# Five warming matmuls in front of the first product, earlier low parts, and other due times in a hybrid decoder layer

## The chip, the cores and the metric

The kernel runs on one core of a Trainium2 chip. The metric is the device time of one execution in microseconds (us). It is measured in several runs, of which the median counts, and once more under the hardware profiler. The engines are named as in the profile: PE (TensorE, its matmuls), PEld (its weight loads), DVE (VectorE), ACT (ScalarE), POOL (GpSimd) and SP (SyncE, which issues most DMAs).

## What is computed

One decoder layer on 512 tokens of width 1024, in float32:

```python
mod = silu(c) @ w_mod + b_mod
shift, scale, gate = split(mod, 3)
h = rmsnorm(x, norm_gain) * (1 + scale) + shift
q, k, v, z_attn, x_lru, z_lru = split(h @ w_in)          # 512 columns each
attn = moba_attention(rope(q), rope(k), v)               # 8 heads x 64; with 512 tokens: causal
y_attn = rmsnorm(attn, attn_out_gain) * silu(z_attn)
rec = rg_lru(causal_depthwise_conv(x_lru))               # gates, then a linear recurrence over time
y_lru = rmsnorm(rec, lru_out_gain) * silu(z_lru)
out = rmsnorm(x + gate * (concat(y_attn, y_lru) @ w_out), final_gain)
```

## The kernel before

Every large product is done with split operands: a number is kept as a rounded part (its name ends in h, type fp32r) and the rest (ends in l), and a product is three matmuls: high by high, low by high, high by low. `split` (L247) issues the high part as a copy, on ACT or DVE, and the low part as a subtraction on DVE.

**The opening.** The input x comes as four tiles of 128 tokens. ACT squares and sums each (L349), and the row is scaled by its inverse norm: the first 256 columns at once (`xs`, L358 and L361), the other 768 later (`x`, L358), not before the time in the table `REST`. The projection's first seven column blocks (q, k and x_lru, `NFIRST`) are accumulated in seven PSUM banks (`acc`) over the eight steps d of the contraction, 128 channels each. For step d:

- two dots on DVE (`gain`, L385 for d = 0, L397 after) take rows of w_mod times silu(c) (`cb`) and give the shift and the scale of these channels; two small instructions (L402, L405) combine them into the columns of `g`. For d > 0 they read `vec`, a table of vectors that a DMA brings, to whose scale columns 1 is added once (L369, on DVE).
- four transposes on PE (L413 from `x`, L417 from `xs` for d = 0) put the tokens along the free axis, in the bank `xp`.
- two ACT instructions (L420) read `xp` and apply `g`: `hh` (rounded) and `h` (full). A subtraction on DVE (L422) gives `hl`.
- the weights' 896 columns are split (`w0dh`, `w0dl`). For d = 0 they come as two pieces of 512 and 384 columns, split apart (`w00512h`, `w00384h` and their low parts).
- 21 matmuls on PE (L432): seven columns by three passes, `hh` with the high weights, `hh` with the low weights, `hl` with the high weights.

Ahead of the first product, matmuls on a constant tile (`warm`) run into a spare bank (`spare`, L312): 24 of them, `NWARM`. PSUM has eight banks, and a tile keeps its bank from its first writer to its last reader.

**The rest.** PE goes through the other column blocks (`UNITS`: x3, four blocks of v, k and q of the second head group, the gates a0 to a3 and l0 to l3), each as 24 matmuls (L243 to L245) into a bank `pj`. Between them stand the attention (scores `sc` L588, softmax on DVE and ACT L601 to L616, transposes `tp` L651, products with v `av` L634) in six blocks, three for each group of four heads, and the recurrence (convolution, gates, `decay`; then `recur`, L547 to L549: a square root on ACT, a product and a scan on DVE for each of four channel blocks). At the end come the output products (`po`, also L243 to L245), the residual and the final norm.

**What sets the order.** The kernel doesn't issue instructions as the code is read. `op` records each with its engine, a cost, what it reads and writes, and a due time or none. `Plan.emit` first works due times back: an operation's due time is the least of its own and, for each that reads its result, that one's due time less its cost and a latency. Then it walks through time by its own clock: on each engine it takes of the operations that could start within 0.12 us of the first the one that is due soonest, adding 4.1 to the due time of an ACT operation that would change the activation table. A tile gets a buffer only when one is free, and no sooner than a window ahead of its due time. The parameter `after` holds an operation back to a time of that clock. What comes out is one fixed order per engine, which the chip follows, waiting on semaphores.

Constants that the change touches: `SPACE` is the distance of the due times of two attention blocks; the second group's first is due at 122.88 on the planner's clock whatever `SPACE` is. `REC0` is the due time of the first recurrence after `T_REST` (50.2). `T_FIRST` (11.8) is the due time of the first product; that of step d is 4.79 d later.

Of the kernel before, what the change touches and what calls it, by code (L numbers as in the profile page):

```python
# [7 lines left out]
F32 = mybir.dt.float32  # L8
F32R = mybir.dt.float32r
BF16 = mybir.dt.bfloat16  # L10
AF = mybir.ActivationFunctionType
OP = mybir.AluOpType
# [5 lines left out]
ND = D // 128  # L18
# [1 line left out]
BIG = 3.0e38  # L20
LRU_C = 8.0
NFIRST = 7
NWARM = 24
CUTS = (((0, 768), (768, 1024)), ((0, 512), (512, 1024)))
REST = (14.6, 14.7, 17.2, 17.3)

V_GAIN, V_SHIFT, V_SCALE, V_GATE = 0, 8, 16, 24
V_CW, V_CB, V_BR, V_BI, V_LAM, V_AG, V_LG = 32, 48, 52, 56, 60, 64, 68
V_C = 72
NV = 80  # L30
UNITS = ["x3", "v0", "v1", "v2", "v3", "k2", "k3", "q2", "q3", "a0", "a1", "l0", "l1", "l2", "l3", "a2", "a3"]
SPACE = 13.0
BY_TANH = ("a0", "a1", "a2", "a3", "l0", "l1", "l2", "l3")
GATE0, GATE_STEP, DECAY0, REC0 = 32.0, 3.0, 56.0, 84.0


class Buf:
# [23 lines left out]
class Plan:  # L61
# [11 lines left out]
    def op(self, eng, cost, fn, r=(), w=(), due=None, table=None, lat=0.25, after=0.0, alt=None):  # L73
        o = Op(eng, cost, fn, list(r), list(w), due, table, lat, after, alt)
        deps = set()
        for b in o.r:
            if b.writer is not None:
                deps.add(b.writer)
        for b in o.w:
            if b.writer is not None:  # L80
                deps.add(b.writer)
            deps.update(b.readers)
        for b in o.r:
            b.readers.append(o)
        for b in o.w:
            b.writer, b.readers = o, []
        for b in set(o.r) | set(o.w):
            b.users += 1
        deps.discard(o)
        o.deps = list(deps)  # L90
        for d in deps:
            d.outs.append(o)
        o.left = len(deps)
        self.ops.append(o)
        return o
# [82 lines left out]
def tile_hymba_block(ctx: ExitStack, tc: tile.TileContext, x, ws0, wss, wgt, win0, wv, winr,  # L178
                     wo, wg, vecs, top, fgain, consts, out):
    nc = tc.nc  # L180
    V, A, G, PE, SP = nc.vector, nc.scalar, nc.gpsimd, nc.tensor, nc.sync
# [19 lines left out]
    op = plan.op  # L201

    def t2(name, dt=F32):
        return Buf("t2", [128, 512], dt, name)

    def t4(name, dt=F32, shape=(128, 1024)):
        return Buf("t4", list(shape), dt, name)

    def bank(name, kind=None):
        return Buf("ps", [128, 512], F32, name, kind)  # L210
# [4 lines left out]
    def fix(name, shape, dt=F32):  # L215
        return Buf("fix", list(shape), dt, name)


    def dv(n, ptr=0):
        return 0.075 + n / 960.0 + 0.06 * ptr  # L220
# [4 lines left out]
    def ac(n, ptr=0, acc=0):  # L225
        return 0.09 + n / 1200.0 + 0.1 * ptr + 0.1 * acc

    def acp(n, ptr=0, acc=0):
        return ac(n, ptr, acc) - 0.039

    def copy(n, dst, src, r, w, due=None, psum=False, after=0.0):

        op("A", acp(n) if psum else ac(n), lambda: A.copy(dst(), src()), r, w, due, after=after,  # L233
           alt=("V", dv(n) if psum else dv2(n), lambda: V.tensor_copy(dst(), src())))

    def pe(n, passes=1):
        return passes * n / 2250.0
# [9 lines left out]
    def split(src, new, name, n, due=None, scale=None, behind=(), late=()):  # L247
        hi, lo = new(name + "h", F32R), new(name + "l", F32R)
        if scale is None:
            copy(n, lambda: hi[:], lambda: src[:], [src, *behind], [hi], due)  # L250
            op("V", dv(n), lambda: V.tensor_sub(lo[:], src[:], hi[:].bitcast(F32)), [src, hi, *late], [lo], due)
        else:
            op("A", ac(n), lambda: A.activation(hi[:], src[:], AF.Copy, scale=scale), [src], [hi], due)
            op("V", dv(n), lambda: V.scalar_tensor_tensor(lo[:], src[:], scale, hi[:].bitcast(F32),
                                                          op0=OP.mult, op1=OP.subtract), [src, hi], [lo], due)
        return hi, lo

    def like(t):
        return lambda name, dt: t4(name, dt, t.shape)


    def t_first(d):
        return T_FIRST + 4.79 * d

    T_FIRST, T_REST, STEP = 11.8, 50.2, 0.94

    def t_step(n):
        return T_REST + STEP * n
# [5 lines left out]
    vec, ident, cst = fix("vec", [128, NV]), fix("ident", [128, 128]), fix("cst", [128, 2048])  # L274
# [34 lines left out]
    warm, spare = t2("warm", BF16), bank("spare")  # L309
    op("V", 0.3, lambda: V.memset(warm[:], 1.0), [], [warm], -10)  # L310
    for n in range(NWARM):
        op("PE", 0.32 if n < 11 else 0.235, lambda: PE.matmul(spare[:], warm[:, 0:128], warm[:], start=True, stop=True),  # L312
# [3 lines left out]
    epsc, ones, junk = fix("epsc", [128, 1]), fix("ones", [128, 1]), fix("junk", [128, 1])  # L316
# [28 lines left out]
    for t in range(NT):  # L345
# [6 lines left out]
        if t > 1:  # L352
            op("V", 0.1, lambda ss=ss: V.reciprocal(ss[:, 0:1], ss[:, 1:2]), [ss], [ss], due + 0.3)
        for dst, cut, e, due2, after in ((xs[t], slice(0, 256), "VVAA"[t], due + 0.4, 0.0), (xt[t], slice(256, D), "A", 20.0 + t, REST[t])):
            o = (lambda d_, c_: d_[:] if d_ in xs else d_[:, c_])
            n = cut.stop - cut.start
# [3 lines left out]
            else:  # L360
# [4 lines left out]
    h = [t2(f"h{d}") for d in range(ND)]  # L365
    hh = [t2(f"h{d}h", F32R) for d in range(ND)]
    hl = [t2(f"h{d}l", F32R) for d in range(ND)]
    acc = [bank(f"acc{j}") for j in range(NFIRST)]
    op("V", 0.1, lambda: V.tensor_scalar(vec[:, V_SCALE:V_SCALE + ND], vec[:, V_SCALE:V_SCALE + ND], 1.0, None,  # L369
                                         op0=OP.add), [vec], [vec], t_first(1) - 3)  # L370

    sch = col("sch")

# [34 lines left out]
    for d in range(ND):  # L408
        g, xp = gain(d), bank(f"xp{d}")

        def turn(xp=xp, d=d):
            for t in range(NT):
                PE.transpose(xp[:, t * 128:(t + 1) * 128], (xt if d > 1 else xs)[t][:, d * 128:(d + 1) * 128], ident[:])  # L413
        if d:
            op("PE", 0.44, turn, (xt if d > 1 else xs) + [ident], [xp], t_first(d) - 3.8)
        for t in range(NT if not d else 0):
            op("PE", 0.11, lambda t=t, xp=xp: PE.transpose(xp[:, t * 128:(t + 1) * 128], xs[t][:, 0:128], ident[:]),  # L417
               [xs[t], ident], [xp], 7 + 0.5 * t)
        for o in (hh[d], h[d]):
            op("A", acp(512, 2), lambda o=o, d=d, xp=xp, g=g: A.activation(  # L420
                o[:], xp[:], AF.Identity, bias=g[:, 0:1], scale=g[:, 1:2]), [xp, g], [o])
        op("V", dv(512), lambda d=d: V.tensor_sub(hl[d][:], h[d][:], hh[d][:].bitcast(F32)), [h[d], hh[d]], [hl[d]])  # L422
        if d:
            wp = [split(w0[d], like(w0[d]), f"w0{d}", 128 * NFIRST)] * 2
        else:
            wp = [split(w, lambda name, dt, w=w: Buf("t2", w.shape, dt, name), w.name, w.shape[1], late=[g],
                        behind=[hh[0]] if w is w0[0][1] else []) for w in w0[0]]
        for i, (a, b) in enumerate(((0, hh[d]), (1, hh[d]), (0, hl[d]))):
            for j in range(NFIRST):
                w, k = wp[j // 4][a], j if d else j % 4  # L430
                op("PE", pe(512), lambda w=w, k=k, b=b, j=j, first=(d == 0 and i == 0), last=(d == ND - 1 and i == 2):
                   PE.matmul(acc[j][:], w[:, k * 128:(k + 1) * 128], b[:], start=first, stop=last),  # L432
                   [w, b], [acc[j]], t_first(d) + (0.62 if d else 1.6) * i + 0.21 * j)
# [290 lines left out]
    for j in range(8):  # L724
# [3 lines left out]
    att = [(g, b) for g in range(2) for b in ((0, 1), (2,), (3,))]  # L728
    t_att = [T_REST + 10.0 + SPACE * n if n < 3 else
             max(t_step(8 * (UNITS.index("q3") + 1)) + 5.0, T_REST + 10.0 + SPACE * 3) + SPACE * (n - 3) for n in range(6)]  # L730
    done = 0
# [57 lines left out]
    for g in range(4):  # L789
# [6 lines left out]
        for j in range(2):  # L796
            w = t4(f"wo{g}{j}", F32, (128, 2, 512))
# [4 lines left out]
        for t in range(NT):  # L802
# [3 lines left out]
            for n, (lo, up) in enumerate(zip(cuts, cuts[1:])):  # L806
                ps, w = bank("po"), up - lo
# [30 lines left out]
                if last and not n:  # L838
# [5 lines left out]
                                                           bias=ssq[t][:, 0:1], scale=1.0 / D), [n4], [n4], t1 + 0.3, "sqrt")  # L844
                op("V", 0.1, lambda t=t: V.reciprocal(ssq[t][:, 3:4], ssq[t][:, 3:4]), [n4], [n4], t1 + 0.4)
                done_a, done_b = Buf("view", None), Buf("view", None)
                for to, up, mark in ((outa[t], 512, done_a), (outb[t], 512, done_b))[:1 if last else 2]:
                    fns = dict(A=lambda t=t, to=to, up=up: A.activation(to[:, :up], to[:, :up], AF.Copy, scale=ssq[t][:, 3:4]),
                               V=lambda t=t, to=to, up=up: V.tensor_scalar(to[:, :up], to[:, :up], ssq[t][:, 3:4], None, op0=OP.mult))
# [86 lines left out]
```

## Time and profile before

| | us |
|---|---|
| three runs | 235.19, 233.93, 235.91 |
| median | 235.19 |
| the profiled execution | 236.3 |
| its span, from the first to the last instruction | 234.2 |

The profile is of one execution. Its page gives busy time for each engine and the granted clock of TensorE in 40 slices; its trace answers for single instructions: when one started, how long it took, and what ended the idle time before it (in square brackets). A matmul's time in a timeline holds its way through the array and so overlaps the next one's; what a matmul costs is the distance of starts. The same holds, by about 0.1 us, for ACT and DVE.

### The profile page before, as it was taken

The page shows a single profiled execution, that of the slowest core. Times are in us where ns is not written, and L with a number is a line of the kernel's source. Part 1 is how long each engine was busy: PE and PEld are TensorE (multiplying, and loading weights), DVE is VectorE, ACT ScalarE, POOL GpSimd, SP SyncE. Part 2 cuts the span into 40 slices and gives each one's busy share as a digit, 9 for nine tenths or more (in the row PEclk, how much of TensorE's full clock was granted, in tenths as well). Part 3 has the DMA queues.
Part 4 walks back from the last instruction along what each step waited for, and adds up shares of the span by engine and source line. Part 5 has one row for each costly group of instructions (what it writes and reads, how often), then busy time and mean ns, then how long its engine had stood idle before and what let it go on. Part 6 is the DMA issues. An engine that isn't in the chain of part 4 may idle for free.

```text
span 234.2 us, 3421 instructions
## 1 busy us (share of the span) xinstructions
PE 224.5 (96%) x1221; PEld 178.2 (76%) x1221; DVE 203.7 (87%) x396; ACT 150.0 (64%) x277; POOL 9.6 (4%) x32
## 2 busy tenths in 40 slices
PE   7969999999999999999999999999999999999990
PEld 3458888888888787686888788778886788888890
DVE  1699998886999997999999999899989999975582
ACT  7888565643549968599998886894763723032363
POOL 1010000067000000000000000000000000000000
PEclk9979999999999999999999999999999999999998
DMA  6999999841270450534322247347450000000044
GB/s 230 395 401 411 404 409 416 347 118 65 71 260 30 179 179 24 206 133 164 108 89 91 94 155 293 96 136 300 189 179 3 0 0 0 3 0 0 0 179 181
DMA packets 11782, 38.27 MB, mean 163 GB/s; under 512 B 1515, under 2 KB 1782, under 8 KB 11638
## 3 DMA queue, kind: packets, MB, share of 16 engines
q1 hardware_dynamic: 11600, 37.80, 43.5%
q10 hardware_dynamic: 166, 0.27, 0.3%
q8 instruction: 9, 0.15, 0.2%
q14 instruction: 7, 0.06, 0.1%
HBM read 35.96 MB, written 2.10 MB: 162 GB/s over the span
## 4 chain that ended last, share of the span: by engine, by line
PE 91%; DMA 3%; DVE 2%; ACT 1%; SPq 1%; issue 0%; ACTq 0%
PE acc L432 17%; PE pj L243 14%; PE pj L245 13%; PE pj L244 13%; PE po L243 6%; PE po L245 6%; PE po L244 6%; PE av L634 4%; PE sc L588 4%; PE tp L651 4%; DMA ws<-in_ws_dram 3%; PE g L511 1%; PE xp L413 1%; DVE ws L385 1%; PE ss L779 1%; SPq L240 1%
## 5 line engine op out<-in xcount | busy, mean ns | idle before, releaser
L604 ACT ACTIVATE z<-z,mn 128x128 f32<-128x128 f32 (+3 forms) x32 | 17.8, 558 | 7.6 <-DVE mn L601 7.5
L397 DVE SCALAR_TENSOR_TENSOR ws<-ws,cb 128x1024 f32<-128x1024 f32 x14 | 16.9, 1221 | 0.5 <-DMA ws<-in_wss_dram 0.5
L601 DVE CUSTOM_DVE_ANT_0 z<-sc,cst 128x128 f32<-128x128 f32 (+3 forms) x32 | 14.3, 486 | 0.9 <-PE pj L244 0.5
L233 ACT COPY pt<-tp 128x128 f32<-128x128 f32 (+3 forms) x28 | 9.7, 405 | 5.5 <-PE tp L651 5.4
L828 ACT ACTIVATE o<-xr 128x512 f32<-128x512 f32 x7 | 4.4, 634 | 12.0 <-DVE xr L817 12.0
L817 DVE SCALAR_TENSOR_TENSOR xr<-po,rba,xr 128x512 f32<-128x512 f32 (+2 forms) x9 | 6.2, 691 | 5.9 <-PE po L245 5.7
L651 PE MATMUL tp<-ident,z 128*128 128x128 f32 x80 | 10.4, 272 | 0.0
L651 PEld LDWEIGHTS tp<-ident,z 128*128 128x128 f32 x80 | 9.3, 141 | 1.3
L799 DVE TENSOR_TENSOR wo<-wo,grow 128x1024 f32<-128x1024 f32 x8 | 9.8, 1219 | 0.0
L559 DVE SCALAR_TENSOR_TENSOR wgt<-wgt,cb 128x1024 f32<-128x1024 f32 x8 | 9.7, 1218 | 0.0
L634 PE MATMUL av<-pt,v 128*64 128x256 f32 (+3 forms) x64 | 9.3, 436 | 0.0
L312 PE MATMUL spare<-warm 128*128 128x512 bf16 x24 | 7.8, 468 | 1.5 <-DVE ones L318 1.5
L634 PEld LDWEIGHTS av<-pt,v 128*64 128x64 f32 x64 | 5.4, 137 | 4.1 <-issue 2.2
L496 DVE SCALAR_TENSOR_TENSOR xc<-xl,vec,xc 128x511 f32<-128x511 f32 (+2 forms) x12 | 8.4, 745 | 0.1
L616 DVE TENSOR_SCALAR z<-z,sum 128x128 f32<-128x128 f32 (+3 forms) x20 | 7.2, 383 | 0.4
L675 ACT ACTIVATE sz<-pj 128x512 f32<-128x512 f32 x8 | 4.8, 599 | 3.7 <-PE pj L245 3.1
L615 ACT ACTIVATE z<-z,sum 128x128 f32<-128x128 f32 (+3 forms) x12 | 6.4, 556 | 0.7 <-DVE sum L612 0.7
L817 DVE SCALAR_TENSOR_TENSOR xr<-po,rbl,xr 128x512 f32<-128x512 f32 x8 | 6.0, 748 | 0.3 <-PE po L245 0.2
L420 ACT ACTIVATE h<-xp,g 128x512 f32<-128x512 f32 x8 | 6.2, 771 | 0.0
L604 ACT ACTIVATION_READ_ACCUMULATOR z<-z,mn 128x1 f32 x32 | 6.1, 190 | 0.0
L312 PEld LDWEIGHTS <-warm 128*128 128x128 bf16 x24 | 2.5, 113 | 4.2 <-DVE ones L318 1.5
L523 DVE COPY gr<-g 64x512 f32<-64x512 f32 x6 | 4.1, 688 | 1.7 <-ACT gi L519 1.6
(1100 smaller groups left out, 752.3 us busy)
## 6 DMA issues: line engine op xcount, KB each, us to landing
wc<-in_winr_dram SPq DMA_DIRECT2D x13, 512.0 KB, 3.4
ws<-in_wss_dram SPq DMA_DIRECT2D x4, 1024.0 KB, 12.1
wgt<-in_wgt_dram SPq DMA_DIRECT2D x8, 512.0 KB, 3.7
wo<-in_wo_dram SPq DMA_DIRECT2D x8, 512.0 KB, 4.2
w<-in_win_dram SPq DMA_DIRECT2D x7, 448.0 KB, 9.5
ws<-in_wss_dram SPq DMA_DIRECT2D x6, 512.0 KB, 6.6
x<-in_x_dram SPq DMA_DIRECT2D x4, 512.0 KB, 5.3
wv<-in_wv_dram SPq DMA_DIRECT2D x4, 512.0 KB, 6.8
```

Source lines behind the costliest of these rows:

```text
L243: PE.matmul(ps, lh, rh, start=start, stop=False)
L244: PE.matmul(ps, lh, rl, start=False, stop=False)
L245: PE.matmul(ps, ll, rh, start=False, stop=stop)
L312: op("PE", 0.32 if n < 11 else 0.235, lambda: PE.matmul(spare[:], warm[:, 0:128], warm[:], start=True, stop=True), [warm], [spare], 5.3 + ...
L397: op("V", dv(1024), lambda j=j: V.scalar_tensor_tensor(part(d, j), part(d, j), 1.0, cb[:], op0=OP.mult, op1=OP.mult, accum_out=sc[:, j:j + ...
L432: PE.matmul(acc[j][:], w[:, k * 128:(k + 1) * 128], b[:], start=first, stop=last),
L601: op("V", dv(n) + 0.085, lambda s=s, z=z, mn=mn: V.tensor_tensor_reduce(out=z[:, :n], in0=ps[s][:, cut], in1=cst[:, 2048 - n:2048], op0=OP ...
L604: op("A", ac(n, 1, 1), lambda s=s, z=z, mn=mn, sm=sm: A.activation(z[:, :n], z[:, :n], AF.Exp, bias=mn[:, 0:1], scale=-1.0, accum_out=sm[: ...
L634: PE.matmul(pss[u][64 * s:64 * s + 64, k * 128:], vt[k][:, h * 64:h * 64 + 64], pts[2 * u + s][:, k, k * 128:], start=(k == 0), stop=(k == 3))
L651: PE.transpose(at(h)[:, k * 128:(k + 1) * 128], z[:, k * 128:(k + 1) * 128], ident[:])
L799: op("V", dv(1024), lambda w=w, s=s: V.tensor_mul(w[:], w[:], grow[:, None, s].to_broadcast([128, 2, 512])), [w, grow], [w], t0 - 7 + 2 * j)
L817: op("V", dv(w, 1), lambda t=t, ps=ps, c0=c0, c1=c1, br=br: V.scalar_tensor_tensor(res[t][:, c0:c1], ps[:, :c1 - c0], rb[br][:, t:t + 1], ...
```

## The change

- `NWARM` goes from 24 to 26, and five more warming matmuls (`NLATE`) are recorded behind the transposes of step 1 (they read its bank `xp`), due from 11.1 on the planner's clock.
- `REST`: the 768 columns of the third and fourth x tile are scaled no sooner than 18.2 and 18.3 on the planner's clock, instead of 17.2 and 17.3.
- The addition of 1 to the scale columns of `vec` goes from DVE (a tensor_scalar) to ACT (an activation with a bias column of ones), due 1 us later.
- `hl` of step 0 gets a due time of 12.5, and the split of the two weight pieces of step 0 one of 12.0; before, these had only what followed from the products.
- `SPACE` goes from 13.0 to 12.6, and `REC0` from 84 to 80.

```diff
@@ -20,18 +20,18 @@
 BIG = 3.0e38
 LRU_C = 8.0
 NFIRST = 7
-NWARM = 24
+NWARM, NLATE = 26, 5
 CUTS = (((0, 768), (768, 1024)), ((0, 512), (512, 1024)))
-REST = (14.6, 14.7, 17.2, 17.3)
+REST = (14.6, 14.7, 18.2, 18.3)
 
 V_GAIN, V_SHIFT, V_SCALE, V_GATE = 0, 8, 16, 24
 V_CW, V_CB, V_BR, V_BI, V_LAM, V_AG, V_LG = 32, 48, 52, 56, 60, 64, 68
 V_C = 72
 NV = 80
 UNITS = ["x3", "v0", "v1", "v2", "v3", "k2", "k3", "q2", "q3", "a0", "a1", "l0", "l1", "l2", "l3", "a2", "a3"]
-SPACE = 13.0
+SPACE = 12.6
 BY_TANH = ("a0", "a1", "a2", "a3", "l0", "l1", "l2", "l3")
-GATE0, GATE_STEP, DECAY0, REC0 = 32.0, 3.0, 56.0, 84.0
+GATE0, GATE_STEP, DECAY0, REC0 = 32.0, 3.0, 56.0, 80.0
 
 
 class Buf:
@@ -366,8 +366,8 @@
     hh = [t2(f"h{d}h", F32R) for d in range(ND)]
     hl = [t2(f"h{d}l", F32R) for d in range(ND)]
     acc = [bank(f"acc{j}") for j in range(NFIRST)]
-    op("V", 0.1, lambda: V.tensor_scalar(vec[:, V_SCALE:V_SCALE + ND], vec[:, V_SCALE:V_SCALE + ND], 1.0, None,
-                                         op0=OP.add), [vec], [vec], t_first(1) - 3)
+    op("A", 0.2, lambda: A.activation(vec[:, V_SCALE:V_SCALE + ND], vec[:, V_SCALE:V_SCALE + ND], AF.Identity, bias=ones[:, 0:1]),
+       [vec, ones], [vec], t_first(1) - 2)
 
     sch = col("sch")
 
@@ -416,14 +416,18 @@
         for t in range(NT if not d else 0):
             op("PE", 0.11, lambda t=t, xp=xp: PE.transpose(xp[:, t * 128:(t + 1) * 128], xs[t][:, 0:128], ident[:]),
                [xs[t], ident], [xp], 7 + 0.5 * t)
+        if d == 1:
+            for n in range(NLATE):
+                op("PE", 0.235, lambda: PE.matmul(spare[:], warm[:, 0:128], warm[:], start=True, stop=True), [warm, xp], [spare],
+                   T_FIRST - 0.7 + 0.1 * n, lat=0.0)
         for o in (hh[d], h[d]):
             op("A", acp(512, 2), lambda o=o, d=d, xp=xp, g=g: A.activation(
                 o[:], xp[:], AF.Identity, bias=g[:, 0:1], scale=g[:, 1:2]), [xp, g], [o])
-        op("V", dv(512), lambda d=d: V.tensor_sub(hl[d][:], h[d][:], hh[d][:].bitcast(F32)), [h[d], hh[d]], [hl[d]])
+        op("V", dv(512), lambda d=d: V.tensor_sub(hl[d][:], h[d][:], hh[d][:].bitcast(F32)), [h[d], hh[d]], [hl[d]], None if d else 12.5)
         if d:
             wp = [split(w0[d], like(w0[d]), f"w0{d}", 128 * NFIRST)] * 2
         else:
-            wp = [split(w, lambda name, dt, w=w: Buf("t2", w.shape, dt, name), w.name, w.shape[1], late=[g],
+            wp = [split(w, lambda name, dt, w=w: Buf("t2", w.shape, dt, name), w.name, w.shape[1], 12.0, late=[g],
                         behind=[hh[0]] if w is w0[0][1] else []) for w in w0[0]]
         for i, (a, b) in enumerate(((0, hh[d]), (1, hh[d]), (0, hl[d]))):
             for j in range(NFIRST):
```

## Rows read from the trace of the kernel before

**Rows 1.** The page: busy time by engine, and the granted clock in 40 slices.

```profile
PE 224.5 (96%) x1221; PEld 178.2 (76%) x1221; DVE 203.7 (87%) x396; ACT 150.0 (64%) x277; POOL 9.6 (4%) x32
...
PEclk9979999999999999999999999999999999999998
```

**Rows 2.** Windows: busy time of each engine, 57 to 227 us.

```profile
sum 170.00, PE 170.00 PEld 136.48 DVE 156.36 ACT 111.90 POOL 1.16; mean PE 85.00 PEld 68.24 DVE 78.18 ACT 55.95 POOL 0.58
```

**Rows 3.** Timeline of PE, 9 to 21 us: start, duration, what, idle time before.

```profile
9.48 1.46 PE L312 MATMUL spare<-warm 128*128 128x512 bf16 x6
11.42 0.33 PE L417 MATMUL xp<-ident,xs 128*128 128x128 f32 x1 [0.47 <-ACT xs L358]
...
12.30 0.60 PE L413 MATMUL xp<-ident,xs 128*128 128x128 f32 x4
14.31 2.08 PE L432 MATMUL acc<-h0h,w00512h 128*128 128x512 f32 x4 [1.41 <-ACT h0h L420]
...
17.47 1.12 PE L432 MATMUL acc<-h0h,w00512l 128*128 128x512 f32 x4
...
20.72 0.84 PE L432 MATMUL acc<-h1h,w01h 128*128 128x512 f32 x3
```

**Rows 4.** The chain that ended last: start, length, what; transposes and a step's products.

```profile
22.47 0.44 PE xp L413 x4
22.91 4.80 PE acc L432 x21
```

**Rows 5.** Windows: length; busy PE, PEld, DVE, ACT, POOL; granted clock; DMA share; GB/s.

```profile
14.00:14.50 0.50, 0.19 (x1) 0.19 (x2) 0.10 (x1) 0.50 (x2) 0.00 (x0) 0.59 0.85 337
...
17.00:17.50 0.50, 0.50 (x3) 0.36 (x2) 0.50 (x3) 0.42 (x1) 0.00 (x0) 0.50 1.07 434
```

**Rows 6.** Timeline of ACT, 13 to 19 us.

```profile
13.48 0.78 ACT L420 ACTIVATE h0h<-xp,g 128x512 fp32r<-128x512 f32 x1
...
14.56 0.78 ACT L420 ACTIVATE h<-xp,g 128x512 f32<-128x512 f32 x1
15.24 1.75 ACT L358 ACTIVATE x<-x,ss 128x768 f32<-128x768 f32 x2
17.08 0.94 ACT L233 CAST w01h<-w 128x896 fp32r<-128x896 f32 x1
17.93 0.94 ACT L358 ACTIVATE x<-x,ss 128x768 f32<-128x768 f32 x1
```

**Rows 7.** Timeline of DVE, 13 to 19 us.

```profile
13.16 0.22 DVE L394 SCALAR_TENSOR_TENSOR g<-sc,v,sch 128x1 f32<-128x1 f32 x1
...
16.19 1.22 DVE L397 SCALAR_TENSOR_TENSOR ws<-ws,cb 128x1024 f32<-128x1024 f32 x1
...
17.34 0.69 DVE L422 TENSOR_TENSOR h0l<-h,h0h 128x512 fp32r<-128x512 f32 x1
17.94 0.17 DVE L369 TENSOR_SCALAR vec<-vec 128x8 f32<-128x8 f32 x1
18.14 0.27 DVE L402 TENSOR_SCALAR g<-sc,vec 128x1 f32<-128x1 f32 x1
18.33 0.15 DVE L405 TENSOR_TENSOR g<-sc,vec 128x1 f32<-128x1 f32 x1
```

**Rows 8.** Timelines: ACT's smallest activation; POOL's wait for the data of vec.

```profile
2.74 0.20 ACT L319 ACTIVATE junk<-epsc 128x1 f32<-128x1 f32 x1
...
14.80 1.09 POOL L443 TENSOR_SCALAR spt<-vec 128x4 f32<-128x4 f32 x1 [13.44 <-DMA vec<-in_vecs_dram]
```

**Rows 9.** Timelines of ACT and PE, 123 to 146 us: table loads, z, its transposes.

```profile
123.94 1.28 ACT L547 ACT_TABLE_LOAD   x1
...
134.06 1.28 ACT L604 ACT_TABLE_LOAD   x1
...
143.97 0.40 ACT L615 ACTIVATE z<-z,sum 128x128 f32<-128x128 f32 x1 [0.43 <-DVE sum L612]
...
145.76 0.60 PE L651 MATMUL tp<-ident,z 128*128 128x128 f32 x4
```

## The prediction

> **What bounds the kernel now.** The page comes first: TensorE is busy for 224.5 of 234.2 us, and of the 40 slices only the third shows a granted clock well under full [rows 1]. The windows after the opening say how strict that is: between 57 and 227 us PE is busy 170.00 of 170.00 us, VectorE 156.36 [rows 2]. Past the opening nothing that only reorders other engines can shorten the time; something is to be won only where PE idles or runs slowly, before 20 us. There the timeline of PE is read next [rows 3]. The last six warming matmuls start at 9.48 and end at 10.94. Then PE has only six transposes until 12.90, and nothing at all until 14.31, when h0h is there. The windows show the clock at 0.59 over 14.00 to 14.50, so it fell at about 14.1 (0.41 us of that half microsecond at half clock make 0.59); it is 0.50, the 1.2 GHz level, still from 17.00 to 17.50 [rows 5], and the four products from 17.47 on, in 1.12 us, go at full clock. So the first seven products take 17.47 - 14.31 = 3.16 us, 0.451 each [rows 3]; at full clock 21 of them take 4.80, 0.2286 each [rows 4]. The penalty is 3.16 - 7 x 0.2286 = 1.56 us.
>
> **The change part by part.** (1) *Five late warmings.* They read xp1, so they stand behind its four transposes, which end at 12.90; the next product waits for h0h until 14.31 [rows 3]. At full clock five cost 5 x 0.243 (1.46 over six) = 1.22 at most, so they end by 14.12 and hide in the 1.41 us of idle time. At half clock they cost 5 x 0.451 = 2.26, end at 15.16 and delay the first product by 0.85. As the clock before fell only around 14.1, I take the first: cost 0, and PE stands still for some 0.2 us instead of 1.41. Whether that is enough to hold the clock no row of before can show. What it wins is bounded by 0 (the clock falls all the same) and the whole 1.56; I take 1.56, since the clock stayed up through everything before 10.94, where warmings stood between transposes in the same way.
> (2) *Two more early warmings.* 2 x 0.243 = 0.49 us, in the 0.47 that PE waits ahead of the transpose at 11.42 [rows 3]. Cost 0; at worst the late chain moves by 0.02.
> (3) *The bank of the warmings.* It is now held to about 14.1 instead of 10.9. With two xp banks it leaves five for the first five products; the sixth takes this bank, and the seventh, at 14.31 + 6 x 0.2286 = 15.68, that of xp0, which is read out when the second h has ended, at 14.56 + 0.78 = 15.34 [rows 6]. Cost 0, with 0.34 to spare.
> (4) *Low parts ahead of the second dot.* With due times of 12.0 and 12.5 against 12.87 for that dot (worked back from the products' due times), DVE takes the low part of the second weight piece, then h0l, then the dot. h0l moves from 17.34 to 16.19 [rows 7]; PE, at full clock, wants it at 14.31 + 14 x 0.2286 = 17.51. In the old order it would end at 17.34 + 0.69 = 18.03, and PE would stand for 0.5 us. The dot starts one slot (17.94 - 17.34 = 0.60) later, at 16.79, and lasts a slot of 17.34 - 16.19 = 1.15, to 17.94. The `vec` addition leaves DVE, so the two g instructions follow at once and are done 0.34 later (18.14 to 18.48), at 18.28.
> (5) *The `vec` addition on ScalarE.* The nearest rows are 0.20 for 128x1 and, far above, 0.78 for 128x512 [rows 6, 8]; I take 0.20, since 8 columns are nearer to 1. Behind it are queued two scalings of x and w01h, for which step 1 waits. Its data lands at 14.80, by POOL's wait [rows 8]. Its due time is 13.8 against 11.6 for the second h, so it goes behind that, at 15.24, and waits for nothing. If it stood ahead of the second weight piece, that piece would be there only at about 15.4 (an estimate: 14.80, 0.20, and 0.4 for the piece, half of w01h's 0.85), for the fifth product at 15.22: PE would lose some 0.2.
> (6) *REST.* Scaling of the third and fourth x is held back to 18.2 on the planner's clock, so h1h no longer stands behind the scaling that starts at 17.93 [rows 6]. ACT is free at 15.24 + 0.20 + 1.84 (two x) + 0.85 (w01h) = 18.13, before g1. h1h starts 0.10 behind g1, as h0h did (13.38 to 13.48): at 18.38. The first product came 0.83 after h0h started, so step 1 can start at 19.21; PE is through step 0 at 14.31 + 21 x 0.2286 = 19.11. Step 1 starts at 19.21 instead of 20.72 [rows 3]: **1.51 us earlier**. Late next is thus h1h, by 0.10. The held-back scalings run from 19.7 to 21.4; the transposes of step 2, which need them, stand some ten products into step 1, at 21.5. A miss costs 0.1.
> (7) *The rest of the opening.* From step 2 on each step has 4.80 of products and 0.44 of transposes on PE, and on DVE two dots, g and two low parts, 2 x 1.15 + 0.34 + 0.60 + 1.0 = 4.2 (the 1.0 an estimate, 0.60 x 896/512). PE stays the later of the two. I lose nothing.
> (8) *Pace 12.6, recurrence due at 80.* No instruction is added: the second attention group's blocks get due times 0.4 and 0.8 us earlier, the square roots, products and scans 4 us. Below nothing there are only switches between sorts of matmul: four transposes among products take 0.60 against 4 x 0.11 in a row [rows 9, 4], so a switch saved or added is about 0.2 us. Above, the price is a PE wait, bounded by the last rival. I take 0: PE has no idle time there to give back, and DVE has 13.6 of 170 us free to absorb a new order [rows 2].
>
> The sum is 1.51. The profiled execution took 236.3 us (span 234.2 and 2.1 around it), so it would take 234.8. It lies 1.1 over the median of 235.19; taken from the median, the sum gives **233.7 us**.
>
> **Rivals.** *The penalty is not whole in every run.* If the clock fell later, or not at all, in some executions of before, the median gains less. For it: the three runs lie 1.98 us apart, somewhat more than the penalty of 1.56, and the profiled execution, which has all of it, is the slowest. Against: only that one execution is seen from inside. With half the gain left, 0.75, the time is 234.4.
> The Trainium skill ("TensorE: Matmul & The Clock Gate", Part 1) has a rule that speaks for this rival: the count of slow matmuls at a kernel's start differs between its runs, 6, 11 or 14 in its example. By that rule the seven of the trace are one draw among several; no row here shows a second one.
> *The clock falls all the same.* Five warmings and a pause may not do. Then (1) wins nothing, and the reorder nothing either, since at half clock PE wants h0l no sooner than it had it; if the clock falls before the five end, the first product is up to 0.85 late. 235.2 to 236.0. For it: the clock did fall with six transposes in the gap. Against: the 1.41 us that were empty are filled.
> *Slower: ScalarE changes tables on softmax's path.* Between 123 and 136 us ACT loads a table four times, first for square roots (123.94), last for the exponentials of the second attention group (134.06), at 1.28 each [rows 9]. Square roots that are due 4 us sooner may go one by one, each as its product is ready, with exponentials between: instead of two pairs four, so two more pairs of loads, 4 x 1.28 = 5.12 us. The last z of the first transposes there is ready at 143.97 + 0.40 = 144.37, and PE takes it at 145.76 [rows 9], 1.39 later. PE would wait 5.12 - 1.39 = 3.7: 233.7 + 3.7 = 237.4. From the third added load on (3.84 - 1.39 = 2.45, over 1.51) the change as a whole is slower. Against it: the planner prices a load, and sooner square roots may as well fall together and spare one.
> The Trainium skill ("ScalarE: Activation LUTs", What ACT_TABLE_LOAD costs) gives 2.66 us for a switch, load and drain together; by that the rival would be 243. The trace differs: the load at 123.94 has no gap on either side, so its 1.28 stands.
>
> **How the numbers follow.** Full gain 0.55 (233.7), partial 0.22 (234.4), none 0.14 (235.2 to 236.0), slower through ScalarE 0.09 (237.4). A change of under 1%, 2.35 us, is about what a measurement of this kernel can't tell from none; the bounds are 232.84 and 237.54. The sum lies 0.8 short of the lower one. Only the spread of the runs, or several spared switches, carries the time past it: 0.14, out of the first case. Past the upper one goes only the larger part of the last case: 0.06. The rest, 0.80, is within. The range goes from 232.6 (1.1 under the first case, half the spread of the runs) to 235.5, into the third case; left out are the last case, part of the third and the tail of the first, under 0.2 together.
>
> **What would show it.** Right: five warming matmuls between 12.9 and 14.1; granted clock 1.00 from 14 to 17.5; seven first products in 1.6 us; h0l at 16.2 on DVE, ahead of the second 1024-wide dot; the `vec` row on ACT behind the second h; step 1 at 19.2; PE's last product ending 1.5 us sooner, with PE busy throughout past the opening. Wrong: a clock of 0.50 after 14 us (the third case), a first product later than 14.31, PE waiting past 57 us for z or for a low part, or more than four table loads on ACT between 120 and 140.

## The result, and the profile after

The changed kernel takes 234.01 us (median of 20 runs, 233.35 to 234.41), the kernel before, measured again beside it, 235.66 (20 runs, 233.93 to 237.89). The ratio is 0.9931, 95% interval 0.9917 to 0.9945: 1.65 us less, where 1.51 was forecast. Runs over 1.5% above the fastest of their kernel count as slow and stand in no ratio: here two of before (237.65 and 237.89; without them it is 1.6 us less), below two of g1. Among the others the scatter fell as well, from 2.53 to 1.06 us, and that turned out to be the more telling number. The profiled execution took 234.14 us, its span 232.1 against 234.2.

The page after, busy time and granted clock in 40 slices, answers to [rows 1]: the 7 in the third slice is gone.

```profile
PE 224.1 (97%) x1228; PEld 176.6 (76%) x1228; DVE 203.1 (88%) x395; ACT 149.8 (65%) x278; POOL 9.6 (4%) x32
...
PEclk9999999999999999999999999999999999999996
```

The timeline of PE after, for [rows 3]: the five warmings (L421) start at 12.65 and end at 13.89, and only 0.33 us are left idle.

```profile
9.29 1.89 PE L312 MATMUL spare<-warm 128*128 128x512 bf16 x8
11.33 0.33 PE L417 MATMUL xp<-ident,xs 128*128 128x128 f32 x1
...
12.65 1.24 PE L421 MATMUL spare<-warm 128*128 128x512 bf16 x5
14.22 1.19 PE L436 MATMUL acc<-h0h,w00512h 128*128 128x512 f32 x4 [0.33 <-ACT h0h L424]
...
15.95 1.08 PE L436 MATMUL acc<-h0h,w00512l 128*128 128x512 f32 x4
...
19.18 0.97 PE L436 MATMUL acc<-h1h,w01h 128*128 128x512 f32 x3
```

The windows after, for [rows 5]; the granted clock is the third number from the end:

```profile
14.00:14.50 0.50, 0.28 (x1) 0.28 (x2) 0.05 (x1) 0.50 (x3) 0.00 (x0) 1.00 0.99 391
...
17.00:17.50 0.50, 0.50 (x4) 0.42 (x3) 0.50 (x1) 0.50 (x2) 0.00 (x0) 1.00 1.02 410
```

The first seven products take 15.95 - 14.22 = 1.73 us instead of 3.16, at full clock, and step 1 starts at 19.18 (forecast 19.21). ACT and DVE after, for [rows 6] and [rows 7], ACT first:

```profile
15.15 0.29 ACT L369 ACTIVATE vec<-vec,ones 128x8 f32<-128x8 f32 x1
15.34 1.76 ACT L358 ACTIVATE x<-x,ss 128x768 f32<-128x768 f32 x2
17.07 0.95 ACT L233 CAST w01h<-w 128x896 fp32r<-128x896 f32 x1
18.35 0.78 ACT L424 ACTIVATE h1h<-xp,g 128x512 fp32r<-128x512 f32 x1 [0.33 <-DVE g L405]
```

```profile
16.17 0.68 DVE L426 TENSOR_TENSOR h0l<-h,h0h 128x512 fp32r<-128x512 f32 x1
16.77 1.22 DVE L397 SCALAR_TENSOR_TENSOR ws<-ws,cb 128x1024 f32<-128x1024 f32 x1
...
17.92 0.27 DVE L402 TENSOR_SCALAR g<-sc,vec 128x1 f32<-128x1 f32 x1
```

h0l at 16.17, the dot at 16.77, g at 17.92 and h1h at 18.35: each within 0.03 of the forecast (16.19, 16.79, 17.94, 18.38).

To compare traces, the execution is cut at five starts of PE instructions: the first product, the first of step 1 (h1h with w01h), the first of the column block x3 (h0h with wc0h), the last matmul, and the end of the span. Before, these stand at 14.31, 20.72, 56.92, 228.09 and 234.2, after at 14.22, 19.18, 55.53, 226.19 and 232.1. All 14 traces by stage, in us:

| kernel | to first product | to step 1 | to x3 | to last matmul | tail |
|---|---|---|---|---|---|
| before | 14.31 | 6.41 | 36.20 | 171.17 | 6.11 |
| after | 14.22 | 4.96 | 36.35 | 170.66 | 5.91 |
| f1, after again | 13.66 | 4.93 | 36.34 | 170.71 | 5.86 |
| e1, no late warmings | 13.51 | 4.95 | 36.34 | 170.66 | 5.94 |
| f2, the same again | 13.55 | 4.93 | 36.32 | 170.71 | 5.89 |
| e2, warmings alone | 14.18 | 5.57 | 36.22 | 171.21 | 5.92 |
| e3, opening alone | 14.11 | 4.97 | 36.49 | 171.83 | 6.00 |
| e4, pace and recurrence alone | 13.93 | 5.55 | 36.21 | 170.80 | 6.11 |
| f3, pace back | 13.84 | 4.95 | 36.35 | 171.10 | 6.16 |
| e5, old order of low parts | 13.46 | 5.32 | 36.20 | 170.86 | 6.06 |
| g1, 20 early, none late | 14.11 | 6.29 | 36.19 | 170.66 | 5.85 |
| g2, 20 early, five late | 14.24 | 5.84 | 36.20 | 170.72 | 5.90 |
| e6, vec on DVE | 14.41 | 5.11 | 36.33 | 170.86 | 5.99 |
| e7, old REST | 14.26 | 5.32 | 36.33 | 171.52 | 5.87 |

The first column scatters by 0.95 us from execution to execution, in no order of the kernels. The fourth repeats within 0.05 where two kernels have the same order past the opening (after, f1, e1, f2). Of the 2.1 us between the profiled spans, 1.45 lie ahead of step 1, and 0.51 behind x3, where I had expected none.

### The profile page after: what moved, and what is told of

Same layout as the page of the kernel before. It is cut to its first block, busy times and chain, and to the rows that moved or that the text cites. A ratio compares the mean times of both kernels' runs of the same rounds, so it can differ in the third digit from the quotient of the medians.

```text
span 232.1 us, 3431 instructions
## 1 busy us (share of the span) xinstructions
PE 224.1 (97%) x1228; PEld 176.6 (76%) x1228; DVE 203.1 (88%) x395; ACT 149.8 (65%) x278; POOL 9.6 (4%) x32
## 4 chain that ended last, share of the span: by engine, by line
PE 91%; DMA 3%; SPq 2%; ACT 1%; DVE 1%; issue 0%; ACTq 0%
PE acc L436 17%; PE pj L243 14%; PE pj L245 13%; PE pj L244 13%; PE po L243 6%; PE po L245 6%; PE po L244 6%; PE av L638 4%; PE tp L655 4%; PE sc L592 4%; DMA w<-in_win_dram 3%; SPq L240 2%; PE g L515 1%; PE xp L413 1%; PE ss L783 1%; ACT h0h L424 0%
## 5 line engine op out<-in xcount | busy, mean ns | idle before, releaser
L233 ACT COPY pt<-tp 128x128 f32<-128x128 f32 (+3 forms) x29 | 10.2, 413 | 4.4 <-PE tp L655 4.4
L638 PE MATMUL av<-pt,v 128*64 128x512 f32 (+3 forms) x64 | 9.1, 436 | 0.0
L638 PEld LDWEIGHTS av<-pt,v 128*64 128x64 f32 x64 | 4.3, 137 | 4.7 <-issue 3.7
L619 ACT ACTIVATE z<-z,sum 128x512 f32<-128x512 f32 (+3 forms) x12 | 6.6, 575 | 1.1 <-DVE sum L616 1.1
L620 DVE TENSOR_SCALAR z<-z,sum 128x256 f32<-128x256 f32 (+3 forms) x20 | 7.0, 376 | 0.3
L680 DVE SCALAR_TENSOR_TENSOR sz<-sz,pj 128x512 f32<-128x512 f32 x8 | 5.5, 683 | 0.8 <-ACT sz L679 0.8
```

The costliest lines, as they stand in the source:

```text
L638: PE.matmul(pss[u][64 * s:64 * s + 64, k * 128:], vt[k][:, h * 64:h * 64 + 64], pts[2 * u + s][:, k, k * 128:], start=(k == 0), stop=(k == 3))
```

## The experiments

**First four, on one chip.** The kernel before, beside them: 235.06 us (34 runs).

e1, the late warmings alone taken out of the changed kernel:

```diff
-NWARM, NLATE = 26, 5
+NWARM, NLATE = 26, 0
```

> The changed kernel without its five late warming matmuls; the order on DVE, ACT and SP is that of the changed kernel, PE's lacks only those five. If the clock makes the gain: granted clock 0.50 from about 14 to 17.5 us, the first seven products in 3.1 to 3.2 us instead of 1.7, step 1 at 20.6 instead of 19.2, and the time 1.4 over the changed kernel, about 235.4. If the earlier low parts on DVE make it: step 1 near 19.2 and 234.0.

Measured: 233.74 us, ratio 0.9958 (0.9935 to 0.9981). The first expectation fell. The second holds, in the time and in the stage to step 1 (4.95 us, as in the changed kernel), but for a reason that it doesn't name. In the profiled execution the clock didn't fall at all; the timeline of PE and two windows of e1:

```profile
9.07 1.89 PE L312 MATMUL spare<-warm 128*128 128x512 bf16 x8
...
11.50 0.60 PE L413 MATMUL xp<-ident,xs 128*128 128x128 f32 x4
13.51 1.21 PE L436 MATMUL acc<-h0h,w00512h 128*128 128x512 f32 x4 [1.41 <-ACT h0h L424]
...
15.25 1.09 PE L436 MATMUL acc<-h0h,w00512l 128*128 128x512 f32 x4
```

```profile
13.50:14.00 0.50, 0.49 (x2) 0.45 (x3) 0.17 (x1) 0.50 (x2) 0.00 (x0) 1.00 1.01 405
14.50:15.00 0.50, 0.50 (x3) 0.39 (x3) 0.50 (x3) 0.50 (x3) 0.50 (x1) 1.00 0.95 381
```

The idle 1.41 us ahead of the first product are those of before, and yet seven products take 1.74 us. But the runs form two groups: eight from 233.17 to 234.42, three from 235.23 to 235.32. Each run's record also has the mean granted clock of TensorE over that execution: 0.991 to 0.997 in the eight, 0.984 to 0.986 in the three. The first seven products at half clock, as in before, would lower such a mean by about 0.5 x 3.16 / 233 = 0.007 (an estimate). So the penalty is a matter of the single execution.

e2, the early and late warmings alone added to the kernel before (`NWARM` 26 and the loop over `NLATE`, nothing else):

> The kernel before with only the two early and five late warming matmuls; DVE, ACT and SP keep the order of before. If clock and order are both needed: full clock, seven products in 1.7 us, then PE stands for 0.5 us before the low part of h at 18.1, step 1 at 19.7, and the time 1.0 under before, about 234.7. If the clock alone carries the gain: step 1 at 19.2 and 234.0. If the clock carries nothing: 235.7.

Measured: 234.80 us, ratio 0.9986 (0.9971 to 1.0002). The first expectation holds in the trace, in its numbers too; PE in e2:

```profile
16.83 0.84 PE L436 MATMUL acc<-h0h,w00384l 128*128 128x512 f32 x3
18.01 1.21 PE L436 MATMUL acc<-h0l,w00512h 128*128 128x512 f32 x4 [0.34 <-DVE h0l L426]
...
19.75 0.62 PE L436 MATMUL acc<-h1h,w01h 128*128 128x512 f32 x2
```

Three products from 16.83 would end at 17.52; PE goes on at 18.01, when h0l is there. In time it wins only 0.26, which its interval doesn't tell from nothing: 25 of the 34 runs of before on this chip have a mean clock of 0.991 or more, and so had no penalty to lose. Its twelve runs lie within 0.77 us (234.48 to 235.25); the 34 of before have 27 from 234.49 to 235.41 and, behind a gap of 0.38, seven from 235.79 to 236.45. Six of those seven, and three of the 27, have a mean clock of 0.983 to 0.990; of e2's twelve none is under 0.991. What the warmings take away is this upper group.

e3, the changed kernel with only its opening changed:

```diff
-SPACE = 12.6
+SPACE = 13.0
-GATE0, GATE_STEP, DECAY0, REC0 = 32.0, 3.0, 56.0, 80.0
+GATE0, GATE_STEP, DECAY0, REC0 = 32.0, 3.0, 56.0, 84.0
```

> The changed kernel with the attention's pace back at 13.0 and the recurrence at 84. If these are worth nothing, as forecast: within 0.15 of the changed kernel, 234.0. If they made the 0.35 us that the changed trace saves between step 1 and the last product beyond the opening: 234.35, with that stretch 206.2 us long again instead of 205.8.

Measured: 234.76 us, ratio 0.9983 (0.9967 to 0.9999). This was the surprise: the opening is as short as after (4.97 to step 1), and nearly nothing is left of it at the end. In time e3 lies 1.11 over the eight runs of e1 that kept the clock (median 233.65). The stretch from x3 to the last matmul is 0.66 longer than before. (The expectation's 206.2 and 205.8 count from step 1 to the first output product of 128 columns; e3 takes 207.1 to there.) PE waits there for a low part of the weights of l2, the tenth block (wc9l); PE and DVE in e3, then DVE and PE after:

```profile
149.58 0.40 PE L244 MATMUL pj<-h0l,wc9h 128*128 128x512 f32 x1
150.35 0.50 PE L245 MATMUL pj<-h0h,wc9l 128*128 128x512 f32 x1 [0.38 <-DVE wc9l L251]
```

```profile
144.00 1.22 DVE L553 TENSOR_TENSOR_SCAN th<-gr,gi 128x512 f32<-128x512 f32 x1
...
148.48 0.68 DVE L680 SCALAR_TENSOR_TENSOR sz<-sz,pj 128x512 f32<-128x512 f32 x1
149.08 1.22 DVE L251 TENSOR_TENSOR wc9l<-wc,wc9h 128x1024 fp32r<-128x1024 f32 x1
```

```profile
141.37 1.22 DVE L553 TENSOR_TENSOR_SCAN th<-gr,gi 128x512 f32<-128x512 f32 x1
...
144.71 1.22 DVE L251 TENSOR_TENSOR wc9l<-wc,wc9h 128x1024 fp32r<-128x1024 f32 x1
```

```profile
148.48 0.39 PE L245 MATMUL pj<-h0h,wc9l 128*128 128x512 f32 x1
```

In e3 the low part starts at 149.08, after the last scan (144.00), a softmax and two waits of DVE for exponentials, and PE, which would go on 0.2286 after 149.58, does so 0.54 later. In the changed kernel the scans are over sooner, the low part starts at 144.71, and PE takes it at 148.48, 2.55 us after it is done. It is the order that loses this, not the earlier opening as such: e2, which keeps the order of before on DVE, ACT and SP, is 0.84 sooner at step 1 and needs 171.21 past x3, as before.

e4, the same two constants changed in the kernel before (13.0 to 12.6, 84 to 80):

> The kernel before with only pace 12.6 and recurrence 80. If these are worth nothing: within 0.2 of before, 235.6, and the stretch from step 1 to the last product 206.2 us. If they save 0.35: 235.3 and 205.8. In both cases the clock falls near 14 us.

Measured: 234.67 us, ratio 0.9976 (0.9957 to 0.9995); the stretch from x3 to the last matmul is 170.80 against 171.17, 0.37 less, so the second expectation holds for the pace. The clock, though, stayed at 1.00 in this trace too, with 24 early warmings and none late. That shows the opening in the order of before at full clock, 19.48 - 13.93 = 5.55 us to step 1, with h0l late for the third pass; PE and a window of e4:

```profile
13.93 1.19 PE L432 MATMUL acc<-h0h,w00512h 128*128 128x512 f32 x4 [1.41 <-ACT h0h L420]
...
17.74 1.21 PE L432 MATMUL acc<-h0l,w00512h 128*128 128x512 f32 x4 [0.34 <-DVE h0l L422]
...
19.48 0.85 PE L432 MATMUL acc<-h1h,w01h 128*128 128x512 f32 x3
```

```profile
14.00:14.50 0.50, 0.50 (x3) 0.42 (x4) 0.27 (x1) 0.50 (x2) 0.00 (x0) 1.00 1.00 397
```

Other executions of e4 did lose it: five of its twelve runs have a mean clock of 0.983 to 0.990, and they are its five longest (234.76 to 235.46).

**Four more, beside the changed kernel.** Before took 234.98 us here (34 runs).

f1 is the changed kernel, f2 is e1 once more:

> The changed kernel itself, beside the next three on one chip. Ratio to before 0.993 as first measured. If the late warmings take away a penalty that only some executions have, its runs lie within 1.2 us of each other with no separate upper group; before has one, about a fifth of its runs, about 1 us up.

> The changed kernel without the five late warmings, again, now beside the changed kernel. If the clock falls in some executions only: most runs within 0.2 of the changed kernel's median, two to four of about eleven 1.4 to 1.6 us above it. If the first run of it was lucky and the penalty is the rule: the median 1.4 above the changed kernel's.

Measured: f1 233.72 us (233.18 to 234.28), ratio 0.9942 (0.9923 to 0.9962); f2 233.85 (233.34 to 234.34), ratio 0.9955 (0.9938 to 0.9972). f1 itself came as expected. f2 has no upper group at all in twelve runs, against three of eleven in e1. Together: in 3 of 23 runs the five late warmings would have been needed. The runs of before here (234.06 to 236.08) show no clear gap, against the expectation, but their clocks divide them: the eleven longest, from 235.52 on, have 0.984 to 0.990, and the other 23, like all of f1 and f2, 0.991 or more.

f3 has the pace alone back at 13.0:

> The changed kernel with the pace alone back at 13.0, recurrence at 80. If the pace is what keeps PE from waiting for the low part of the tenth weight block: that wait of about 0.5 us is back, and the time is 0.7 over the changed kernel. If the sooner recurrence does it: as the changed kernel, within 0.2.

Measured: 233.89 us, ratio 0.9959 (0.9941 to 0.9977). No PE wait for wc9l; the stretch from x3 on is 171.10, between e3's 171.83 and the changed kernel's 170.7. So in the new opening the sooner recurrence is worth 0.73 there, and the pace, on top of it, 0.4. In time, 0.17 over f1, within the scatter.

e5 takes the two due times off the low parts of step 0:

```diff
-    ... [hl[d]], None if d else 12.5)
+    ... [hl[d]])
-    ... w.shape[1], 12.0, late=[g],
+    ... w.shape[1], late=[g],
```

> The changed kernel without the two due times for step 0's low parts, so that its second dot goes ahead of the low part of h. By the prediction's step 4: low part of h at 17.3 instead of 16.2, PE stands for 0.5 us ahead of the third pass, first product to step 1 in 5.5 instead of 4.96 us, and the time 0.5 to 0.6 over the changed kernel. If the transposed chain of g sets step 1 anyway: no more than 0.1.

Measured: 233.66 us, ratio 0.9953 (0.9932 to 0.9974). The trace shows the wait, PE's third pass of e5 held up until 17.06 (three products from 16.11 would end at 16.80):

```profile
16.11 0.84 PE L436 MATMUL acc<-h0h,w00384l 128*128 128x512 f32 x3
17.06 1.19 PE L436 MATMUL acc<-h0l,w00512h 128*128 128x512 f32 x4
...
18.78 0.84 PE L436 MATMUL acc<-h1h,w01h 128*128 128x512 f32 x3
```

5.32 to step 1 instead of 4.93: 0.39 of the 0.5 expected. The median shows none of it (233.66 against 233.72), the ratio some 0.3 us (0.9953 against 0.9942, with intervals that overlap). Past x3 the planner's order differs from f1's too (170.86 against 170.71). Its first product came at 13.46 in the profiled execution and that column scatters by more than 0.39, so the runs can't tell; what the order is worth is read from the traces alone.

**The last four.** Before took 235.57 us here (31 runs).

g1 and g2 lengthen the stretch without warmings, the one without and the other with the late ones:

```diff
-NWARM, NLATE = 26, 5
+NWARM, NLATE = 20, 0
```

(g2: 20, 5.)

> The changed kernel with 20 early warming matmuls instead of 26 and no late ones, so that PE has only transposes from about 9.8 us on; the order on DVE, ACT and SP is that of the changed kernel. If the clock falls more surely the longer the stretch without warmings is: it falls in most executions, the seven first products take 3.1 us, first product to step 1 is 6.4 instead of 4.95 us, and the median is 1.4 over the changed kernel, 235.2. If the clock rarely falls whatever is done in the opening: 233.8.

> The same with 20 early and the five late warming matmuls. If the late ones alone hold the clock: as the changed kernel, 233.7, first product to step 1 in 4.95 us, no upper group of runs. If they come too late after a longer pause: they take 0.43 us each, the first product is 0.5 us or more later and the median lies between 234.3 and 235.5.

Measured: g1 235.71 us, ratio 0.9985 (0.9953 to 1.0017), two runs at 233.06 and 233.22, then ten from 235.18 to 236.87. g2 234.62, ratio 0.9956 (0.9936 to 0.9976), 233.42 to 235.02. PE and two windows of g1, then of g2:

```profile
9.33 0.59 PE L312 MATMUL spare<-warm 128*128 128x512 bf16 x2
11.21 0.33 PE L417 MATMUL xp<-ident,xs 128*128 128x128 f32 x1 [1.28 <-ACT xs L358]
...
14.11 2.07 PE L436 MATMUL acc<-h0h,w00512h 128*128 128x512 f32 x4 [1.41 <-ACT h0h L424]
...
17.19 1.09 PE L436 MATMUL acc<-h0h,w00512l 128*128 128x512 f32 x4
```

```profile
13.00:14.00 1.00, 0.00 (x0) 0.00 (x0) 0.87 (x2) 0.93 (x3) 0.00 (x0) 0.83 0.97 387
14.00:15.00 1.00, 0.89 (x2) 0.79 (x3) 0.59 (x1) 1.00 (x3) 0.35 (x1) 0.50 1.03 413
```

```profile
12.58 2.23 PE L421 MATMUL spare<-warm 128*128 128x512 bf16 x5
14.24 2.13 PE L436 MATMUL acc<-h0h,w00512h 128*128 128x512 f32 x4
16.22 0.85 PE L436 MATMUL acc<-h0h,w00384h 128*128 128x512 f32 x3
```

```profile
12.00:13.00 1.00, 1.00 (x7) 0.77 (x8) 0.96 (x5) 0.36 (x1) 0.00 (x0) 0.84 1.03 394
13.00:14.00 1.00, 1.00 (x4) 0.35 (x3) 0.91 (x2) 0.94 (x3) 0.00 (x0) 0.50 1.06 402
```

In g1 the clock falls around 13.7 and the penalty is whole: 6.29 to step 1, 1.33 over the changed kernel's 4.96 (which has no runs on this chip). This execution, 235.18 us with a mean clock of 0.990, is the shortest of the ten. Seven of them have 0.977 to 0.980, lower than any run of before, and take 235.66 to 236.87: that points to a clock that was down for longer than here, but no trace shows such an execution. In g2 it falls as the late warmings begin (0.84 over 12 to 13, 0.50 after); they take twice their time, and the first four products come at half speed: 5.84, 0.9 over. The first product is late by 0.09 only: 0.92 behind h0h, which starts at 13.32, instead of 0.83. So the five late matmuls don't hold the clock by themselves: with 26 early ones ahead of them the runs of after and f1 show no upper group, with 20 the clock fell in the trace, and the runs reach from 233.42 to 235.02.

Over all runs that have a mean clock on record, those at 0.990 or less:

| warmings early, late | kernels | runs |
|---|---|---|
| 24, 0 | before on three chips, e4 | 39 of 111 |
| 26, 0 | e1, f2 | 3 of 23 |
| 26, 5 | after, f1, e2, e3, f3, e5, e6, e7 | 1 of 95 |
| 20, 0 | g1 | 10 of 12 |
| 20, 5 | g2 | 7 of 12 |

The three traces in which the clock fell in the opening (before, g1, g2) have 0.989 to 0.990, the other eleven 0.991 to 0.996. The mean also holds a fall behind the last matmul, which every trace has, so a single run at 0.990 or 0.991 can be either; the one of 95 is such a run, 234.54 us in e3. The two more early warmings seem to have their part beside the five late ones, since the order on DVE, ACT and SP ahead of the first product is the same in all these kernels; that isn't tested singly, as no run has 24 early and five late.

e6 puts the addition to `vec` back on DVE, e7 sets `REST` back to 17.2 and 17.3:

> The changed kernel with the addition to the vector table back on DVE. By the prediction's step 4: g of step 1 is ready 0.2 later, so h1h at 18.55 instead of 18.35 and first product to step 1 in 5.1 instead of 4.95 us; the time 0.1 to 0.2 over the changed kernel, within what the runs can tell. If the activation had cost ScalarE something that step 1 waits for: 0.1 to 0.2 under.

> The changed kernel with the old times for scaling x, so that the third scaling goes ahead of h1h. It starts at about 18.0 and holds ACT for 0.85: h1h at 18.85 instead of 18.35, first product to step 1 in 5.45 instead of 4.95 us, the time 0.5 over the changed kernel. If something else sets step 1: no more than 0.1.

Measured: e6 234.07 us, ratio 0.9932 (0.9909 to 0.9955); e7 234.83, ratio 0.9973 (0.9950 to 0.9997). To step 1 e6 needs 5.11 (0.15 more, as expected) and e7 5.32 (0.36 of the 0.5 expected); ACT in e7 shows the scaling that h1h stands behind:

```profile
17.93 0.93 ACT L358 ACTIVATE x<-x,ss 128x768 f32<-128x768 f32 x1
18.77 0.76 ACT L424 ACTIVATE h1h<-xp,g 128x512 fp32r<-128x512 f32 x1
```

e7's loss is larger in time than there: its stretch from x3 on is 171.52, 0.86 over the changed kernel. The planner's order past the opening came out differently. One row of it is a wait of PE for DVE, 0.40 us, in e7; what makes the other half is open:

```profile
101.32 0.63 PE L655 MATMUL tp<-ident,z 128*128 128x128 f32 x4 [0.40 <-DVE pt L234]
```

## Why the prediction was right, and where it wasn't

The sum was right: 1.51 forecast, 1.65 at first and 234.98 - 233.72 = 1.26 beside f1; 233.7 forecast, 234.01 and 233.72 measured. Its parts hold for the profiled pair: 6.41 - 4.96 = 1.45 ahead of step 1. But the sum is not made of what I said.

- *Steps (1) and (2), the clock.* The size was right for an execution in which the clock falls. The step that failed is to take this execution for all: e1, f2 and e4, without late warmings, kept full clock in their traces, and in 20 of 23 runs of e1 and f2 nothing was lost. The first rival's condition is thus met. In the order of before the price is also smaller than 1.56: at full clock h0l keeps PE waiting (e4: 5.55 to step 1), so the fall costs 6.41 - 5.55 = 0.86. The runs agree: on the three chips the runs of before with a mean clock of 0.990 or less have a median 0.9 to 1.2 above that of the rest.
- *Step (4), the order on DVE.* Right in each start, and its worth rises to first place: 5.55 - 4.96 = 0.59 in an execution at full clock, together with (5) and (6). With the clock down it is 6.41 - 6.29 = 0.12 (before and g1). Undone singly the three cost 0.39, 0.15 and 0.36 in the traces.
- *Steps (3), (5), (6).* As forecast; the activation took 0.29 and held ACT for 0.19.
- *Step (7).* Step 1 to x3 is 0.15 longer than before, a loss that was put at nothing. Most of it lies in the first three products of step 1, 0.97 us from 19.18 against 0.84 from 20.72.
- *Step (8), pace and recurrence at 0.* Wrong twice, and with it the premise that past the opening no new order can shorten the time. Alone they save 0.37 past x3 (e4). And without them the kernel would have lost 0.66 there (e3): with the new opening the planner, at the old due times, comes to an order in which DVE has the low part of the tenth block ready at 149.08 + 1.22 = 150.30 for a PE that wants it at 149.81. The changed kernel is 171.83 - 170.66 = 1.17 better in that stretch than e3. I had read "PE busy 170.00 of 170.00" as no time to give back. But a matmul's busy time holds its way through the array, 0.39 us where it costs 0.2286, and covers short waits: of e3's 0.54 the timeline shows 0.38 as idle, and stretches of 171.17 and 170.66 look equally full in such a window. No PE row past x3 shows idle time, before or after. Added up by starts, the products there take 139.93 us instead of 140.28 (21 unbroken stretches instead of 22), the products with v 8.91 instead of 9.17, the transposes 8.07 instead of 7.92 (11 groups instead of 10): so the 0.51 is won in what the matmuls cost in the new order, and not in idle time. Why the products with v got cheaper is open. My price of 0.2 for a switch of sorts was misread too, from the busy time of 0.60 of four transposes. By starts these take 146.12 - 145.76 = 0.36 and the product behind them 0.31, together 0.67, which is no more than 4 x 0.11 + 0.2286:

```profile
146.12 0.48 PE L243 MATMUL pj<-h5h,wc8h 128*128 128x512 f32 x1
146.43 0.40 PE L244 MATMUL pj<-h5l,wc8h 128*128 128x512 f32 x1
```

- *The rival on ScalarE's tables.* It didn't come. Between 120 and 140 us there are four loads as before (first 121.64, last 131.59): the four square roots still go in two groups, now three and one instead of two and two. What did take the opening's gain back, where the constants were left alone, was another engine, DVE, through the order that the planner gave it.

So the first rival was right in its mechanism and wrong in its sum: with the penalty absent from most executions the median would have gained little from the warmings alone (e2: 0.26), but the order on DVE (0.59) and the retimed middle (0.51) filled its place. Beside f1, the 23 runs of before that kept the clock have a median of 234.57, so 0.85 of the 1.26 stay when no clock falls, and some 0.4 are the clock's share of the median. That these came to the forecast sum is luck.

ACT's loads after, first and last of the four:

```profile
121.64 1.28 ACT L551 ACT_TABLE_LOAD   x1
...
131.59 1.28 ACT L608 ACT_TABLE_LOAD   x1
```

## What to carry to other kernels

Where a planner makes the order, an edit at the start also reorders the middle, and may lose there what it wins: compare stage by stage, by the starts of a few marked instructions rather than by PE's busy share, and expect that due times further down have to move too. A penalty seen in one profiled execution may be there in an eighth of the runs or in most (3 of 23, 10 of 12); the spread of the runs, whether they form groups, and the mean granted clock of each tell more of it than one trace. Here warming matmuls earned little in the median and much in the spread, and the five in the pause did it with 26 early ones ahead of them, not with 20.

## What the runs showed of the hardware

Whether the clock falls differs from execution to execution of nearly the same opening. From the end of the last early warming to the first product, with six transposes on PE in between and no late warmings, 3.37 us passed in before (10.94 to 14.31, the clock fell), 3.25 in e4 (10.68 to 13.93, it did not), 2.55 in e1 (10.96 to 13.51, it did not), 1.98 in f2 (11.57 to 13.55, it did not) and 4.19 in g1 (9.92 to 14.11, it fell, as in ten of its twelve runs by their times). The Trainium skill ("TensorE: Matmul & The Clock Gate", Part 1) says of a kernel's start that the number of slow matmuls differs from run to run. Here the slow ones, seven in before, seven in g1 and none in e1, f2 and e4, come behind a stretch at full clock; that runs of one kernel differ, e1's mean clocks show.

The time of the first product scatters from 13.46 to 14.41 us over fourteen traces that have the same instructions ahead of it on DVE, ACT and SP, and it passes into the end of the execution undiminished: the four stages behind it add up to 217.84 to 217.89 us in after, f1, e1 and f2. Differences of less than half a microsecond between kernels therefore stand in the stages of the traces, and not in medians of a dozen runs.
